# Dealing the prompt's chunks to five blocks: 5, 7, 7, 7, 6 in place of 4, 7, 7, 7, 7

## The chip, the core and the metric

The kernel runs on one core of a Trainium2 chip. The metric is device time in microseconds (us); a run's time is one execution of the whole kernel, and medians of several runs are compared. PE is TensorE's matmul, PEld its weight load, DVE is VectorE, ACT is ScalarE, POOL is GpSimd, SP is SyncE, whose queue issues most transfers. The profiled execution is one run by itself.

## What is computed

One layer of a streaming encoder for two groups of tokens: a sample of 64 tokens that continues a running stream, and a prompt of 2048 tokens with 16 meta tokens in front. Each row of 1024 values is normalised, projected to 11144 columns, and sent through three branches; their gated sum is projected again, added to the input and normalised:

```python
P   = x @ w_in                       # 11144 columns
y_b = branch_b(P columns) * silu(gate_b columns)      # b in rwkv7, s5, mlstm
m   = sum_b sigmoid(P_merge_b + b_merge_b) * (y_b @ w_br_b)
x   = layer_norm(DN_ALPHA * x + m @ w_out)
```

RWKV-7 carries a 64 x 64 state in each of 12 heads, S5 a complex diagonal state in 32 groups, mLSTM a 192 x 192 memory in each of 4 heads. Every branch is causal by token, so tokens can be worked in chunks with the state carried over. All states are outputs, for the sample and for the prompt. Everything is float32.

## The kernel before, in words

The 64 + 16 + 2048 = 2128 tokens lie in one row, cut into five **blocks** (BLOCKS, L36, a number of 64-token chunks for each). Block 0 holds the sample, the meta tokens and four chunks of the prompt: T = 336 columns. The others hold seven chunks, 448 columns. Activations are held with features on the partitions and tokens along the free dimension, so that T is the width of nearly every instruction.

A float32 product is made of three matmuls on parts (mm3, L427): weight and activation are each split into a high and a low part, and for each of eight slices of 128 input features there are three matmuls, 24 for 128 output columns. There are 63 such projections per block (psum tile d) and 24 for the merge gates (gate_pass, L1493, mostly psum tile f). In block 0 (`first`) the weights come from w_in: split_w (L392) loads a tile (wraw, graw), casts it on ACT (L403), subtracts on POOL (L404) and stores both parts in memory (wsp, L409); load_w (L414) of later blocks loads these parts (L423). Buffers: three of wraw, four each of whi and wlo, two each of graw, ghi and glo. The normalised activations xh, xl of a block stand in one set of buffers, loaded from xT for each block after the first.

RWKV works in **slots** of 64 tokens: block 0 has a slot for the sample, one for the meta tokens (48 of its 64 places empty) and one for each chunk, six in all; the other blocks have seven. For each of six head pairs, rw_front (L512) makes the operands and inverts a triangular block for all slots at once (L615, L617, 31 steps whatever the number of slots), rw_prep (L628) makes slot matrices with small matmuls, and rw_back (L715) runs the state from slot to slot (L723, L741) and normalises.

mLSTM works in **token tiles** of up to 128 (Block.tiles). In block 0 they are 64 (sample), 16 (meta), 128, 128; in the others 128, 128, 128, 64. ml_tiles (L976) runs through them one after the other, for each of two head pairs, and carries the memory Cst; the scale factors per tile are made in ml_gates (L834). ln_first (L205) normalises block 0 in the same tiles, all of them kept in memory before the first projection; ln_stage (L168) does it for the next block while a block runs, and stores xT. Both load a tile's rows with one transfer (src_rows, L158). S5 (s5_block, L1310) works on T/8 columns with scans; its tables are made once, in block 0's time (s5_setup, L1119, mostly L1128).

The order of the work is not that of the program text alone. Generators of the three branches are interleaved by weights (mix, L1449; MIXES, L1671), and a planner then places every instruction on its engine with simulated times. The last RWKV pair, the second mLSTM head pair and S5 of block 0 are finished in the next block's time (pend, mpend, spend).

After the last block, merge_pass (L1503) works on the 2112 tokens without the meta rows in groups of 768, 768 and 576 (TBS, L1504): branch outputs (yraw) and gates (th) are loaded for each group, one transfer for each block that the group touches (segs), then three branch products and the output product (L1556) and the last norm (norm) follow. Its groups end at 768 and 1536; block borders lie at 320, 768, 1216 and 1664 of the same count.

Of the kernel before, what the change touches and what calls it, by code (L numbers as in the profile page):

```python
# [21 lines left out]
NMETA = 16  # L22
NSAMP = 64
NTOK = NSAMP + NMETA + SEQ
# [8 lines left out]
DN_ALPHA = 2 ** 0.25  # L33
O_RW, O_RG, O_S5U, O_S5G, O_MQ, O_MK, O_MV, O_MIF, O_MO, O_MZ, O_MG = (
    0, 2432, 3200, 3712, 4224, 4992, 5760, 6528, 6536, 7304, 8072)
BLOCKS = (4, 7, 7, 7, 7)  # L36
CH = 64
C2 = 0.5 * math.exp(-0.5)
LN05 = math.log(0.5)
# [2 lines left out]
HPO = 300  # L42
TMAX = CH * max(BLOCKS)
RMAX = 448
# [3 lines left out]
class Block:  # L48
    def __init__(self, i, t0, nch):
        self.i, self.t0, self.nch = i, t0, nch  # L50
        self.first = i == 0
        pre = NSAMP + NMETA if self.first else 0
        self.T = pre + CH * nch
        self.nslot = nch + (2 if self.first else 0)
        self.R = self.nslot * CH
        self.last = i == len(BLOCKS) - 1
        if self.first:
            self.seqs = [(0, NSAMP), (NSAMP, self.T - NSAMP)]
            self.pads = [(0, 0, 80), (80, 128, self.T - 80)]
            self.shift = [(0, 0, 64, 0), (64, 64, 16, 1), (80, 128, self.T - 80, 1)]  # L60
            self.tiles = [(0, 64), (64, 16)]
        else:
            self.seqs = [(0, self.T)]
            self.pads = [(0, 0, self.T)]
            self.shift = [(0, 0, self.T, 0)]
            self.tiles = []
        t = pre
        while t < self.T:
            n = min(128, self.T - t)
            self.tiles.append((t, n))  # L70
            t += n


def make_blocks():
    out, t = [], 0
    for i, n in enumerate(BLOCKS):
        b = Block(i, t, n)
# [6 lines left out]
def tile_trunk(ctx: ExitStack, tc: tile.TileContext, I, O, dbg=None, parts=("rw", "s5", "ml", "mg")):  # L84
    nc = tc.nc
# [21 lines left out]
    def pt(pool, shape, tag, dt=F32, bufs=None):  # L107
        uid[0] += 1
        kw = {} if bufs is None else {"bufs": bufs}
        return pool.tile(list(shape), dt, tag=tag, name=f"{tag}_{uid[0]}", **kw)  # L110
# [3 lines left out]
    def psum(shape, tag):  # L114
        return pt(ps, shape, tag, bufs=PSB[tag])
# [9 lines left out]
    def flat(tag, n, dt=F32, bufs=None):  # L125
        return pt(op, (128, n), tag, dt, bufs=bufs)

    def cut(t, off, shape):
        n = 1
        for x in shape[1:]:  # L130
            n *= x
        v = t[:shape[0], off:off + n]
        if len(shape) == 3:
            v = v.rearrange("p (a b) -> p a b", b=shape[2])
        elif len(shape) == 4:
            v = v.rearrange("p (a b c) -> p a b c", b=shape[2], c=shape[3])
        elif len(shape) == 5:
            v = v.rearrange("p (a b c d) -> p a b c d", b=shape[2], c=shape[3], d=shape[4])
        return v
# [15 lines left out]
    SB = 4  # L155
    NX = 1536

    def src_rows(b, lo, n):  # L158
        g = b.t0 + lo
        if g < NSAMP:  # L160
            return I["x_sample"][0, g:g + n, :]
        g -= NSAMP
        if g < NMETA:
            return I["meta"][g:g + n, :]
        g -= NMETA
        return I["x_prompt"][0, g:g + n, :]

    def ln_stage(b):  # L168
        for i, (lo, n) in enumerate(b.tiles):
            X = flat("X", NX)  # L170
            x = cut(X, 0, (128, D))
            nc.sync.dma_start(x[:n], src_rows(b, lo, n))
            st = pt(lnp, (128, 2, 6), "st", bufs=2)
            for j in range(2):
                V.bn_stats(st[:n, j, :], x[:n, 512 * j:512 * j + 512])
            mv = pt(lnp, (128, 2), "mv", bufs=2)
            V.bn_aggr(mv[:n], st[:n])
            ve = pt(lnp, (128, 1), "ve", bufs=2)
            V.tensor_scalar(ve[:n], mv[:n, 1:2], 1.0, LN_EPS, ALU.mult, ALU.add)
            rs = pt(lnp, (128, 1), "rs", bufs=2)  # L180
            rsqrt(lnp, rs[:n], ve[:n], (n, 1), "lq")
            nb = pt(lnp, (128, 1), "nb", bufs=2)
            V.scalar_tensor_tensor(nb[:n], mv[:n, 0:1], -1.0, rs[:n], ALU.mult, ALU.mult)
            S.activation(x[:n], x[:n], AF.Identity, bias=nb[:n], scale=rs[:n])
            for j in range(2):
                p = psum((128, 4, 128), "o")
                for k in range(4):
                    c0 = 512 * j + 128 * k
                    PE.transpose(p[:, k, :n], x[:n, c0:c0 + 128], ident[:n, :n])
                for k in range(0, 4, 2):  # L190
                    kk = 4 * j + k
                    xg = cut(X, 1024, (128, 2, 128))
                    hi = cut(X, 1280, (128, 2, 128)).bitcast(F32R)
                    for i in range(2):
                        V.tensor_scalar(xg[:, i, :n], p[:, k + i, :n], pcol("in_g", kk + i), pcol("in_b", kk + i),
                                        ALU.mult, ALU.add)
                    S.copy(hi[:, :, :n], xg[:, :, :n])
                    G.tensor_tensor(xg.bitcast(F32R)[:, :, :n], xg[:, :, :n], hi.bitcast(F32)[:, :, :n], ALU.subtract)
                    nc.sync.dma_start(xT_d[b.i][0, :, kk:kk + 2, lo:lo + n], hi.bitcast(F32)[:, :, :n])
                    nc.scalar.dma_start(xT_d[b.i][1, :, kk:kk + 2, lo:lo + n], xg[:, :, :n])  # L200
            yield
# [3 lines left out]
    def ln_first(b):  # L205
        nt = len(b.tiles)
        xs = []
        mv = pt(lnp, (128, nt, 2), "mv4")
        V.memset(mv, 1.0)
        for i, (lo, n) in enumerate(b.tiles):  # L210
            X = flat("va", NVA) if i == 0 else flat("X", NX) if i == 3 else pt(
                rp, (128, NSL, 2, 128), "AT", bufs=2).rearrange("p c h t -> p (c h t)")
            x = cut(X, 0, (128, D))
            nc.sync.dma_start(x[:n], src_rows(b, lo, n))
            st = pt(lnp, (128, 2, 6), "st", bufs=2)
            for j in range(2):
                V.bn_stats(st[:n, j, :], x[:n, 512 * j:512 * j + 512])
            V.bn_aggr(mv[:n, i], st[:n])
            xs.append((x, cut(X, 1024, (128, 4, 128))))
        ve = pt(lnp, (128, nt), "ve4")  # L220
        V.tensor_scalar(ve, mv[:, :, 1], 1.0, LN_EPS, ALU.mult, ALU.add)
        rs = pt(lnp, (128, nt), "rs4")
        rsqrt(lnp, rs, ve, (128, nt), "lq4")
        nb = pt(lnp, (128, nt), "nb4")
        V.scalar_tensor_tensor(nb, mv[:, :, 0], -1.0, rs, ALU.mult, ALU.mult)
        cur["xh"], cur["xl"] = ([pt(big, (128, TMAX), f"{nm}{k}", F32R) for k in range(KD)] for nm in ("xh", "xl"))
        for i, (lo, n) in enumerate(b.tiles):
            x, xg = xs[i]
            if str(i) in NV:
                V.tensor_scalar(x[:n], x[:n], rs[:n, i:i + 1], nb[:n, i:i + 1], ALU.mult, ALU.add)  # L230
            else:
                S.activation(x[:n], x[:n], AF.Identity, bias=nb[:n, i:i + 1], scale=rs[:n, i:i + 1])
            for j in range(2):
                p = psum((128, 4, 128), "o" if j or not NP else "d")
                for k in range(4):
                    c0 = 512 * j + 128 * k
                    PE.transpose(p[:, k, :n], x[:n, c0:c0 + 128], ident[:n, :n])
                for k in range(4):
                    kk = 4 * j + k
                    hi, l = cur["xh"][kk][:, lo:lo + n], cur["xl"][kk][:, lo:lo + n]  # L240
                    S.activation(hi, p[:, k, :n], AF.Identity, bias=pcol("in_b", kk), scale=pcol("in_g", kk))
                    V.tensor_scalar(xg[:, k, :n], p[:, k, :n], pcol("in_g", kk), pcol("in_b", kk), ALU.mult, ALU.add)
                    G.tensor_tensor(l, xg[:, k, :n], hi.bitcast(F32), ALU.subtract)
        for j, nm in enumerate(("xh", "xl")):
            for k in range(KD):
                nc.sync.dma_start(xT_d[b.i][j, :, k, :], cur[nm][k].bitcast(F32)[:, :b.T])
# [65 lines left out]
    def pcol(name, j=0, n=1):  # L312
        return PT[:, col[name] + j:col[name] + j + n]
# [5 lines left out]

    load_rows(0, 2, ["rk"])  # L320
    ln_first(blocks[0])
    load_rows(2, len(rows_spec), ["kk", "L", "Bc"])

# [1422 lines left out]
```

## Time and profile before

| | |
|---|---|
| median of 3 runs | 4168.24 us (4159.67 to 4174.69) |
| profiled execution | 4180.76 us, of which the span from the first to the last instruction is 4179.0 us |
| PE busy | 3882.8 us, 93% |
| DVE busy | 2513.7 us, 60% |
| ACT busy | 1206.4 us, 29% |
| POOL busy | 672.2 us, 16% |
| moved by DMA | 834.88 MB, 200 GB/s on the mean |
| mean granted clock of TensorE | 0.958 |

Busy is the time in which an engine had an instruction; matmuls are pipelined, so one lasts longer than the distance to the next, and a stream's pace is read from the starts. The granted clock is a share of 2.4 GHz, the mean of a stretch over the levels 1.2 and 2.4 GHz. In the 40 slices of the page, POOL is busy in the first six (block 0) and the last six (merge), where weights are split.

### The profile page before, as it was taken

What the parts mean: (1) busy time and instruction counts of PE and PEld (TensorE: products, weight loads), DVE (VectorE), ACT (ScalarE), POOL (GpSimd) and SP (SyncE); (2) the same over time, 40 slices, a digit from 0 to 9 for tenths busy, and PEclk for the clock granted to TensorE, in tenths of its full rate; (3) what the DMA queues carried; (4) which work ended last, traced back from release to release, by engine and by line L of the source; (5) the groups of instructions that cost most, each with busy time, mean ns of one, the idle gap of its engine ahead of it and who ended that gap; (6) DMA issues with size and microseconds to landing.
All of it is one profiled execution on the core that took longest, in us unless ns stands there. A gap on an engine that the chain in (4) does not pass through costs nothing.

```text
span 4179.0 us, 78015 instructions
## 1 busy us (share of the span) xinstructions
PE 3882.8 (93%) x27729; PEld 3321.6 (79%) x27729; DVE 2513.7 (60%) x8212; ACT 1206.4 (29%) x2655; POOL 672.2 (16%) x978
## 2 busy tenths in 40 slices
PE   6888779899999899999899999999999998999997
PEld 6777567687888788788778888778888786999997
DVE  6556887566566555656545656564666554357476
ACT  5334332233222222223222322232322232222222
POOL 5544322000000000001000001000000000232334
PEclk9999879899999899999999999999999999999999
DMA  8999647665666755666655656566565556566565
GB/s 265 314 288 313 214 132 230 181 200 184 189 212 199 238 180 182 194 186 209 190 191 176 199 184 214 174 214 204 176 204 186 158 169 183 169 197 194 160 179 161
DMA packets 803860, 834.88 MB, mean 200 GB/s; under 512 B 220246, under 2 KB 557374, under 8 KB 803470
## 3 DMA queue, kind: packets, MB, share of 16 engines
q1 hardware_dynamic: 725582, 756.61, 58.4%
q10 hardware_dynamic: 77888, 73.28, 6.0%
q8 instruction: 219, 3.59, 0.4%
q14 instruction: 171, 1.40, 0.1%
HBM read 633.92 MB, written 197.79 MB: 199 GB/s over the span
## 4 chain that ended last, share of the span: by engine, by line
PE 61%; DMA 11%; DVE 9%; SPq 2%; ACT 2%; issue 1%; POOL 1%; ACTq 0%; DVEq 0%; POOLq 0%
PE d L432 25%; PE f L432 8%; PE z L1556 7%; PE g L1556 3%; DMA xT<-X 2%; PE py L723 1%; DMA ghi<-wsp 1%; PE tr L578 1%; PE d L1411 1%; DMA E<-rd 1%; PE tr L697 1%; PE tr L705 1%; DMA Uin<-Ud 1%; PE o L1005 1%; PE o L1368 1%
## 5 line engine op out<-in xcount | busy, mean ns | idle before, releaser
L432 PE MATMUL d<-xh,whi 128*128 128x448 f32 (+1 forms) x2520 | 951.4, 378 | 31.4 <-ACT X L935 9.6
L432 PE MATMUL d<-xh,wlo 128*128 128x448 f32 (+1 forms) x2520 | 940.0, 373 | 7.5 <-POOL wlo L404 6.9
L432 PE MATMUL d<-xl,whi 128*128 128x448 f32 (+1 forms) x2520 | 933.8, 371 | 0.0
L432 PEld LDWEIGHTS d<-xh,whi 128*128 128x128 f32 x2520 | 489.1, 194 | 89.6 <-issue 14.0
L432 PEld LDWEIGHTS d<-xh,wlo 128*128 128x128 f32 x2520 | 488.3, 194 | 60.8 <-POOL wlo L404 11.2
L432 PEld LDWEIGHTS d<-xl,whi 128*128 128x128 f32 x2520 | 489.1, 194 | 44.5 <-issue 8.5
L404 POOL TENSOR_TENSOR wlo<-wraw,whi 128x512 fp32r<-128x512 f32 (+1 forms) x310 | 399.5, 1298 | 541.8 <-ACT whi L403 505.0
L432 PE MATMUL f<-xh,ghi 128*128 128x448 f32 (+1 forms) x912 | 351.2, 385 | 42.3 <-DMA ghi<-wsp 17.0
L432 PE MATMUL f<-xh,glo 128*128 128x448 f32 (+1 forms) x912 | 346.5, 380 | 14.5 <-POOL glo L404 10.3
L432 PE MATMUL f<-xl,ghi 128*128 128x448 f32 (+1 forms) x912 | 340.5, 373 | 0.0
L403 ACT CAST whi<-wraw 128x512 fp32r<-128x512 f32 (+1 forms) x310 | 179.2, 585 | 400.5 <-PE z L1556 111.5
L615 DVE TENSOR_TENSOR Ztmp<-Uin,Z 128x60 f32<-128x60 f32 (+24 forms) x930 | 214.0, 230 | 99.5 <-DMA Uin<-Ud 84.4
L432 PEld LDWEIGHTS f<-xh,ghi 128*128 128x128 f32 x912 | 180.0, 197 | 72.6 <-ACT ghi L403 18.6
L617 DVE TENSOR_TENSOR Z<-Z,Ztmp 128x60 f32<-128x60 f32 (+24 forms) x930 | 213.5, 230 | 15.6
L432 PEld LDWEIGHTS f<-xh,glo 128*128 128x128 f32 x912 | 179.6, 197 | 41.5 <-POOL glo L404 14.2
L1556 PE MATMUL z<-ya,whi 128*128 128x384 f32 (+1 forms) x784 | 192.1, 325 | 0.0
L432 PEld LDWEIGHTS f<-xl,ghi 128*128 128x128 f32 x912 | 180.5, 198 | 13.4 <-issue 2.0
L942 DVE SCALAR_TENSOR_TENSOR X<-X,PT 128x448 f32<-128x448 f32 (+1 forms) x180 | 123.0, 683 | 55.0 <-ACT X L940 53.0
L1556 PEld LDWEIGHTS z<-ya,whi 128*128 128x128 f32 x784 | 138.1, 189 | 0.2 <-issue 0.2
L1500 ACT ACTIVATE gt<-f,hbm 128x448 f32<-128x448 f32 (+1 forms) x114 | 69.9, 613 | 200.4 <-PE f L432 142.0
L1556 PE MATMUL z<-ya,wlo 128*128 128x384 f32 (+1 forms) x384 | 124.9, 325 | 0.0
L1556 PE MATMUL z<-yb,whi 128*128 128x288 f32 (+1 forms) x512 | 119.8, 316 | 2.7 <-DVE lq2i L251 1.8
(724 smaller groups left out, 6866.9 us busy)
## 6 DMA issues: line engine op xcount, KB each, us to landing
whi<-wsp SPq DMA_DIRECT2D x504, 256.0 KB
wlo<-wsp SPq DMA_DIRECT2D x504, 256.0 KB
ghi<-wsp SPq DMA_DIRECT2D x192, 256.0 KB
glo<-wsp SPq DMA_DIRECT2D x192, 256.0 KB
wraw<-in_w_in_dram SPq DMA_DIRECT2D x126, 256.0 KB
wsp<-whi SPq DMA_DIRECT2D x126, 256.0 KB
wsp<-wlo SPq DMA_DIRECT2D x126, 256.0 KB
gt<-gt SPq DMA_DIRECT2D x96, 224.0 KB
```

Of the source, the lines that this page charges most:

```text
L403: S.copy(h[:, :n, :M], raw[:, :n, :M])
L404: G.tensor_tensor(l[:, :n, :M], raw[:, :n, :M], h.bitcast(F32)[:, :n, :M], ALU.subtract)
L432: PE.matmul(p, a[k], c, start=i == 0, stop=i == 3 * KD - 1)
L578: i = PE.matmul(p[h][:, c].rearrange("p (j t) -> p j t", j=2), bk[h][:, c0 + c, :], AQ[hs[h], c0 + c], start=True, stop=True)
L615: V.tensor_tensor(t3, Uin[:, j:j + 1, j + 1:32].to_broadcast((128, m, n)), Z[:, 0:m, j:j + 1].to_broadcast((128, m, n)), ALU.mult)
L617: V.tensor_tensor(Z[:, 0:m, j + 1:32], Z[:, 0:m, j + 1:32], t3, ALU.add)
L697: PE.matmul(p[hs[h], c], Tt[hs[h], c0 + c, :], AR[hs[h], c0 + c], start=True, stop=True)
L705: PE.matmul(p[hs[h], c], PX[hs[h], c0 + c, 0, :], AT[hs[h], c0 + c, h, :], start=True, stop=True)
L723: i = PE.matmul(o, a, x, start=start, stop=stop, skip_group_check=True)
L942: V.scalar_tensor_tensor(acc[:, :w], raw[:, j:j + w], pcol("conv_w", 12 * j + ti), acc[:, :w], ALU.mult, ALU.add)
L1500: S.activation(t[:, :T], p[:, :T], AF.Tanh, scale=0.5, bias=hbm[:, j:j + 1])
L1556: PE.matmul(p, a[k], c[:, sl], start=i == 0, stop=i == n - 1)
```

## The change

The list becomes (5, 7, 7, 7, 6). Block 0 then has 400 columns and seven slots, the last block 384 columns and six slots; the blocks in between keep their size and begin one chunk later. Block 0's tiles after the sample are no longer cut at the end of the meta rows: they are 64, 128 (16 meta rows and 112 of the prompt), 128 and 80; the last block's are 128, 128, 128. A tile can thus have its rows in two inputs; load_rows_x issues a transfer for each and takes the place of src_rows in ln_stage and ln_first.

```diff
-BLOCKS = (4, 7, 7, 7, 7)
+BLOCKS = (5, 7, 7, 7, 6)
...
-            self.tiles = [(0, 64), (64, 16)]
+            self.tiles = [(0, 64)]
...
-        t = pre
+        t = NSAMP if self.first else 0
...
-    def src_rows(b, lo, n):
...
+    def load_rows_x(x, b, lo, n):
+        parts_ = ((0, I["x_sample"][0]), (NSAMP, I["meta"]), (NSAMP + NMETA, I["x_prompt"][0]))
+        g, i = b.t0 + lo, 0
+        for (s0, src), s1 in zip(parts_, (NSAMP, NSAMP + NMETA, NTOK)):
+            m = min(g + n, s1) - max(g + i, s0)
+            if m > 0 and g + i >= s0:
+                nc.sync.dma_start(x[i:i + m], src[g + i - s0:g + i - s0 + m, :])
+                i += m
...
-            nc.sync.dma_start(x[:n], src_rows(b, lo, n))
+            load_rows_x(x, b, lo, n)
```

Block borders in the count without meta rows move to 384, 832, 1280 and 1728.

## Rows read from the trace of the kernel before

**Rows 1.** The page: busy shares, and the group of weight loads of one kind.
```profile
PE 3882.8 (93%) x27729; PEld 3321.6 (79%) x27729; DVE 2513.7 (60%) x8212; ACT 1206.4 (29%) x2655; POOL 672.2 (16%) x978
...
L432 PEld LDWEIGHTS d<-xh,whi 128*128 128x128 f32 x2520 | 489.1, 194 | 89.6 <-issue 14.0
```
**Rows 2.** Stretches: length, busy PE, PEld, DVE, ACT, POOL, clock, DMA share, GB/s.
```profile
30.00:440.00 410.00, 352.39 (x2339) 314.68 (x2337) 238.93 (x708) 161.97 (x352) 199.91 (x219) 0.93 0.95 305
440.00:683.00 243.00, 183.07 (x1341) 145.63 (x1341) 201.86 (x860) 84.82 (x236) 72.06 (x107) 0.78 0.56 172
...
2860.00:3430.00 570.00, 556.16 (x4223) 461.82 (x4223) 350.69 (x1159) 160.22 (x361) 29.88 (x84) 0.99 0.58 178
...
3567.00:4179.00 612.00, 578.98 (x3594) 572.33 (x3592) 360.14 (x657) 148.19 (x244) 226.43 (x180) 0.98 0.59 174
```
**Rows 3.** The same stretches, L432 alone: length, busy PE, PEld, clock, DMA.
```profile
30.00:440.00 410.00, 303.25 (x1631) 270.77 (x1629) 0.93 0.95 305
440.00:683.00 243.00, 95.79 (x457) 84.12 (x457) 0.78 0.56 172
...
2860.00:3430.00 570.00, 389.12 (x1680) 310.83 (x1680) 0.99 0.58 178
3430.00:3567.00 137.00, 88.29 (x360) 67.23 (x360) 0.96 0.63 189
```
**Rows 4.** The chain's shares in 440:700, 2860:3430, 3430:3570 and 3570:4179.
```profile
by line: DVE sB L1128 7.8%; PE d L432 6.4%; DMA s5wo<-sB 3.5%; DVE X L942 3.4%; DVE Ztmp L615 2.9%; PE o L1277 2.3%; DVE Z L617 2.2%; PE f L432 2.2%; DVE sA L1128 2.0%; issue 1.7%; DMA Kd<-tab 1.2%; PE tr L578 1.1%; DMA Uin<-Ud 1.0%; PE tr 
...
by line: PE d L432 45.2%; PE f L432 4.9%; DMA E<-rd 2.9%; PE py L723 2.6%; PE tr L578 2.5%; PE tr L705 1.8%; PE tr L697 1.7%; DMA Uin<-Ud 1.5%; PE o L1005 1.2%; issue 1.2%; DMA Tt<-Zd 1.1%; PE o L1375 1.1%; PE tr L711 1.1%; PE d L1411 1.1%;
...
by line: PE f L432 20.5%; DMA ghi<-wsp 18.7%; PE d L432 14.9%; DMA glo<-wsp 10.3%; SPq L633 2.3%; DMA Uin<-Ud 2.3%; PE py L723 2.1%; DVE Ztmp L615 2.0%; PE z L1556 2.0%; PE o L1005 2.0%; DVE Z L617 1.9%; PE o L1000 1.8%; issue 1.5%; PE tr L
...
by line: PE z L1556 48.9%; PE g L1556 23.0%; DMA yraw<-yml 4.2%; issue 2.4%; DVE st L1590 1.7%; DVE xn L1599 1.7%; DVE lq2a L255 1.6%; DMA wraw<-in_w_out_dram 1.6%; DVE lq2a L254 1.5%; DMA xr<-xT 1.4%; DVE xn L1600 1.4%; DVE rs L260 1.4%; P
```
**Rows 5.** Pieces of the chain: start, length, what.
```profile
1494.33 9.85 PE d L432 x48
...
3466.02 4.54 DMA glo<-wsp
...
3567.33 134.41 PE z L1556 x768
...
4046.95 47.97 PE z L1556 x360
```
**Rows 6.** PE's groups by shape, whole span: count, busy, mean ns; idle before.
```profile
L578 PE MATMUL tr<-AQ,BK 64*128 64x128 f32 x816 | 91.4, 309 | 4.0 <-DVE BK L560 2.5 <-POOL BK L561 1.5
...
L1005 PE MATMUL o<-Cst,t 128*64 128x193 f32 x40 | 10.2, 335 | 0.0
...
L723 PE MATMUL py<-Ss,AQ 64*64 64x64 f32 x96 | 8.2, 249 | 0.2 <-ACT Ss L789 0.2
...
L1065 PE MATMUL o<-ident,NK 64*128 64x64 f32 x30 | 4.6, 244 | 0.0
```
**Rows 7.** What SP's queue waited for in 3430:3567: total, times, longest.
```profile
SPq L423 <- PE f L432: 39.5, 13, 6.5
```
**Rows 8.** PE in order of time in 305:311 (block 0): start, length.
```profile
304.74 0.32 PE L432 MATMUL f<-xh,glo 128*128 128x336 f32 x1
...
308.94 0.31 PE L432 MATMUL d<-xh,wlo 128*128 128x336 f32 x1
```
**Rows 9.** A DVE group in 440:683: count, busy, mean ns.
```profile
L604 DVE SCALAR_TENSOR_TENSOR sg<-sg,d 128x336 f32<-128x336 f32 x3 | 1.5, 497 | 1.4 <-ACT sg L603 1.4
```
**Rows 10.** The same group in 2860:3567.
```profile
L604 DVE SCALAR_TENSOR_TENSOR sg<-sg,d 128x448 f32<-128x448 f32 x6 | 3.7, 613 | 1.8 <-ACT sg L603 1.8
```
**Rows 11.** Transfers in 30:440.
```profile
DMA packets 138059, 124.85 MB, mean 305 GB/s; under 512 B 18015, under 2 KB 102968, under 8 KB 138019
```
**Rows 12.** The start in order of time, DVE's statistics of two tiles.
```profile
6.89 1.26 DVE L217 BATCH_NORM_STATS2 st<-AT 16x6 f32<-16x512 f32 x2
...
8.31 1.27 DVE L217 BATCH_NORM_STATS2 st<-AT 128x6 f32<-128x512 f32 x2
```

More of the change, by code (lines that the diff above doesn't have):

```diff
@@ L156, in tile_trunk @@
     NX = 1536
-    def src_rows(b, lo, n):
[L159 to L166, printed above, removed]
+    def load_rows_x(x, b, lo, n):
[6 more added lines that the diff above has]
+                i += m
     def ln_stage(b):
@@ L213, in ln_first @@
             x = cut(X, 0, (128, D))
-            nc.sync.dma_start(x[:n], src_rows(b, lo, n))
+            load_rows_x(x, b, lo, n)
             st = pt(lnp, (128, 2, 6), "st", bufs=2)
```

## The prediction, written before the result

> **What bounds the kernel now.** I read the page's busy shares first, then cut the span into stages, then asked in each stage which wait ends last. TensorE is busy for 93% of the span [rows 1], so its idle places decide what work can be moved for nothing. The stages show where these are [rows 2]: the reader compares the PE column with the length of each stretch. From 30 to 440 us PE idles 410 − 352 = 58 us, and there the DMA engines are taken for 95%; from 440 to 683 us it idles 243 − 183 = 60 us, the granted clock is 0.78, a mixture of the 1.2 and 2.4 GHz levels, and VectorE is busy for 202 of the 243 us. From 2860 to 3430 us PE idles only 14 of 570 us.
>
> The first two stretches are block 0: the matmuls of L432 in them are 1631 + 457 [rows 3], which is the 87 × 24 = 2088 of one block (63 projections and 24 merge gates, 24 matmuls each). The next two are the last block (2040 of its 2088). So block 0 waits for something other than PE, and the last block waits for PE. The chain says the same [rows 4]: in 440 to 700 us its first name is VectorE's L1128 (the tables of S5), from 2860 to 3430 us it is L432 with 45%. From 3430 to 3570 us the chain alternates between L432 and the weight loads (ghi, glo).
>
> **The change part by part.** One chunk of 64 tokens moves from the last block to block 0. Block 0 goes from 336 to 400 columns and from 6 to 7 slots, the last block from 448 to 384 columns and from 7 to 6 slots. Totals stay (336 + 448 = 400 + 384), so the worth of the change is the difference between the price of a chunk where PE is the limit and its price where it is not.
>
> *Off the last block, PE work.* (a) Projections and gates. 48 matmuls of 448 columns follow each other in 9.85 us, 205 ns each; in the merge, 768 of 384 columns take 134.4 us, 175 ns each; 360 of 288 columns take 48.0 us, 133 ns each [rows 5]. The spacing follows the columns. 2088 × (205 − 175) = 62.6 us, of which 360 × 30 = 10.8 us lie after 3430 us. (b) One slot of the RWKV work. The twelve groups of small matmuls with one entry per slot (L578, L723, L697, L705, L689, L684, L711, L668, L659) are busy for 507 us over 6 + 4 × 7 = 34 slots [rows 6], 14.9 us a slot. (c) Two mLSTM tiles: 448 tokens are tiles of 128, 128, 128, 64; 384 are three of 128; there are two head pairs. The eleven groups of 64-row tiles are busy for 71.9 us in ten passes [rows 6], 7.2 us each, 14.4 us for two. (d) Transposes that go from four to three per pass and S5's eight columns fewer: a few us, left at nothing. The sum is 62.6 + 14.9 + 14.4 = 92 us.
>
> At a spot of the Trainium skill this sum would be far smaller. Its page TensorE: Matmul & The Clock Gate (Back-to-back issue gap) gives for a stream of weight loads and matmuls about 81 ns per matmul at 128 columns and about 131 ns at 512, a slope of 0.13 ns per column; as an estimate from that page, 64 columns would be worth 8.3 ns and (a) 17 us. The rows above have 0.44 to 0.47 ns per column, so the measurement decides and (a) stays.
>
> How much of the 92 us shortens the block? Not more than all. The least is half: PE is busy for 97.6% from 2860 to 3430 us, but the matmuls named in the chain's row there add up to 63% (small groups left out); the rest holds round trips (E, Uin, Tt from memory [rows 4]) that other generators' matmuls cover and that show up when the cover gets thinner. After 3430 us the load of the next gate's weights waits for the matmuls that read the buffer (39.5 us in 13 waits [rows 7]) and lands some 4.5 us later [rows 5], so a shorter matmul group shortens about half of each round. VectorE, busy for 351 of 570 us, is late next, but far off. I take 80%, nearest to the busy share: −73 us, between −46 and −92.
>
> *Onto block 0.* PE gets 2088 × 29 ns (64 columns at 155.6/336 = 0.46 ns each: 27 spacings in 4.20 us [rows 8]) = 60.6 us, plus 14.9 us for the slot: 76 us, against 118 us of idle time. By the counts of rows 3, 78% of it, 59 us, falls into 30 to 440 us where 58 are idle, 17 us into 440 to 683 us where 60 are idle (at the low level of the clock it would be up to 34). The cover is the DMA stream in the first stretch and VectorE in the second; if PE had to pay, it would be 76 us.
> VectorE: the same instruction (L604) takes 497 ns at 336 columns and 613 ns at 448 [rows 9, 10], 1.04 ns a column, 66 ns for 64. Some 300 instructions per block have that width (read from the code): 20 us. In the first stretch VectorE is busy for only 239 of 410 us, so that part is hidden; in the second it is the limit, and its share by time (243 of 653 us) is 7 us. I take it as exposed.
> DMA: 64 more columns of x, xT, gates and branch outputs are about 2.5 MB (gates 3072 × 64 × 4 = 0.8 MB, x and both halves of xT 0.8 MB, branches about 0.9 MB). At the stretch's 305 GB/s [rows 11] that is 8 us, exposed because the queue has no room there.
> Another 5 us are for PE where it happens to be the later one. Sum: 7 + 8 + 5 = 20 us, between +5 and +60.
>
> *The rest.* The tile of 16 meta rows grows into a full one across the border, and a last tile of 80 rows comes in: block 0's four tiles stay four. The small tile was not cheap for being small: statistics of 16 rows take 1.26 us, of 128 rows 1.27 us [rows 12]. The border tile needs two loads; block 0's start gets 1 us, between 0 and 3. Of block 0's deferred work (second head pair of mLSTM, last RWKV pair, S5) block 1 gets 64 columns more on a full PE: +3 us, between 0 and 8. The blocks in between shift by one chunk and keep size. In the merge the second group of 768 tokens is now cut from three blocks instead of two: 16 + 24 + 16 = 56 more transfers, most of them pieces of 64 columns, on SP's and ACT's queues. PE is busy for 579 of 612 us there and the waits for yraw are 4.2% of it, 26 us [rows 4], so +2 us, between 0 and 8. Those on ACT's queue stand before the casts of ACT, which is busy for 148 of 612 us.
>
> Sum: −73 + 20 + 1 + 3 + 2 = −47 us. The profiled execution took 4180.8 us (span 4179.0), so 4134 us; it stands 12.5 us above the median of the runs, 4168.2, so I predict 4121 us. A change below 0.3%, 12.5 us, can't be told from none here.
>
> **Rivals.**
> *Block 0 hides nearly everything* (over −70 us): PE really fits, VectorE's 7 us fall between its waits, and the last block gives 92: −92 + 8 = −84, 4084 us. For it: 118 us of idle PE. Against: both stretches have a second resource near its limit.
> *The weight load sets the spacing.* A load of 128 columns lasts 194 ns on the mean [rows 1]. Were a matmul of 384 columns held to that, (a) would be 2088 × 11 = 23 us and the block would lose 23 + 29 = 52 × 0.8 = 42 us: −42 + 26 = −16, 4152 us. Against: the merge's 288 columns run at 133 ns [rows 5]. Small.
> *The DMA stream takes over all of it.* The extra bytes, VectorE and a thinner cover cost 45 us in block 0 and the last block gives only its half: −46 + 45 + 6 = +5, 4173 us, no change.
> *Slower: the weight buffers tie PE and DMA together in block 0.* A new weight tile is loaded, cast on ACT, subtracted on POOL, and both parts are stored; its buffers (four of whi and wlo, two of ghi and glo) come free only after the matmuls that read them. If every group of 24 matmuls holds them 0.7 us longer and the DMA engines pause meanwhile, PE's 59 us add to the 410 us instead of filling them, the 17 to 34 us add to the second stretch, with VectorE's 7: +83 to +100 us. That decides from the point where block 0 grows by more than 67 us; at +90 it is −73 + 90 + 6 = +23, 4191 us. For it: 95% DMA with PE idle in pieces, which is how such a ring looks. Against: a share of 95% leaves no pause to be longer.
> That the change doesn't do what it says can't be: the column counts follow from the list. But the order of all instructions is planned anew, and that alone may move the end by some 10 us either way.
>
> **How the numbers follow.** Forecast (−15 to −70 us) 0.62; block 0 hides nearly everything 0.15; weight load 0.03; no change 0.12; slower 0.08. Range: 4080 us (the second case, a little beyond) to 4165 us (the upper end of the forecast and most of the third); about 0.2 lie outside. Faster by over 0.3%: 0.62 + 0.15 + 0.02 = 0.79; within: 0.12; slower: 0.09.
>
> **What would show it.** L432 at about 175 ns in the last block and 183 ns in block 0; the first 448-wide matmul about 20 us later than 683 us; the stretch from there to the merge's first matmul about 70 us shorter; PE's idle time in block 0 well below 118 us, VectorE near its limit in the last third. I would be wrong if block 0 grew by over 67 us, or if the last block kept its length with PE idle.

## The result and the profile after

The changed kernel takes 4117.3 us (median of 4 runs, 4111.6 to 4120.8) against 4164.0 us before in the same group of runs: ratio 0.9883, 95% interval 0.9864 to 0.9902, 47 us less. Run again in the group of the experiments it came to 0.9906 (0.9886 to 0.9925), 39 us. The forecast was −47 us and 4121 us. The profiled execution took 4111.6 us, 69 us less than that of before; of these some 22 us are chance, for the profiled execution of before was slower than its median and this one was the fastest of its four.

In the changed kernel's text one line is gone above the places named, so L432 is L431, L1556 is L1555, and so on. The page's busy shares; PE is busy for 43 us less in all:

```profile
PE 3839.6 (93%) x27644; PEld 3330.6 (81%) x27644; DVE 2483.5 (60%) x8127; ACT 1201.7 (29%) x2626; POOL 686.3 (17%) x974
```

The stretches of [rows 2] in the changed kernel, the last two of them with the new borders (length, busy PE, PEld, DVE, ACT, POOL, granted clock, DMA share, GB/s):

```profile
30.00:440.00 410.00, 380.07 (x2426) 345.63 (x2425) 259.44 (x738) 173.69 (x359) 205.58 (x226) 0.98 0.94 303
440.00:683.00 243.00, 193.32 (x1394) 159.16 (x1394) 204.38 (x837) 86.58 (x227) 70.94 (x107) 0.85 0.62 190
...
2844.00:3372.00 528.00, 504.67 (x3847) 448.89 (x3846) 293.71 (x1087) 141.73 (x340) 32.27 (x81) 0.96 0.66 206
3372.00:3506.00 134.00, 102.16 (x831) 87.47 (x830) 65.80 (x235) 38.56 (x91) 4.28 (x7) 0.84 0.53 147
3506.00:4110.00 604.00, 577.66 (x3592) 571.49 (x3591) 359.66 (x658) 148.38 (x244) 229.35 (x180) 0.99 0.60 177
```

Against [rows 2] the reader sees PE filling its idle time in block 0 (352 to 380 us, 183 to 193 us), at a granted clock that rose from 0.93 to 0.98 and from 0.78 to 0.85, and a new weak place: from 3372 us to the merge PE is busy for 102 of 134 us at a clock of 0.84. In the 134 us ahead of the merge of before it was 118 us at 0.96:

```profile
3433.00:3567.00 134.00, 118.39 (x771) 95.22 (x771) 62.33 (x237) 38.27 (x91) 0.80 (x2) 0.96 0.63 187
```

Where a block ends is read from counts: 2088 matmuls of L432 (L431) belong to each. L432 before, and then L431 after, each cut where four blocks are done and where the merge begins (length, busy PE, PEld, clock, DMA):

```profile
0.00:2844.00 2844.00, 1862.70 (x8352) 1523.67 (x8352) 0.95 0.67 209
2844.00:3567.00 723.00, 488.88 (x2088) 386.66 (x2088) 0.98 0.60 184
```
```profile
0.00:2845.00 2845.00, 1895.95 (x8352) 1555.23 (x8352) 0.97 0.68 211
2845.00:3505.50 660.50, 430.26 (x2089) 372.81 (x2088) 0.94 0.63 194
```

8352 is 4 × 2088. The first four blocks, one of them now a chunk longer, end 1 us later than before. The last block takes 660 us instead of 723, and the merge 604 instead of 612. So in this pair of executions the chunk costs about nothing where it went and gives 62 us where it came from. Cut in the same way after each of the first four blocks, with all engines (columns as in [rows 2]), before and after:

```profile
0.00:681.50 681.50, 542.16 (x3693) 465.37 (x3695) 461.14 (x1658) 263.21 (x628) 287.81 (x381) 0.88 0.80 251
681.50:1399.00 717.50, 684.72 (x5255) 567.84 (x5255) 452.32 (x1671) 198.64 (x458) 44.34 (x114) 0.98 0.66 202
1399.00:2140.00 741.00, 700.76 (x5121) 579.92 (x5122) 419.32 (x1429) 195.22 (x431) 39.57 (x105) 0.95 0.62 193
2140.00:2844.00 704.00, 682.63 (x4938) 564.01 (x4938) 403.40 (x1383) 196.86 (x433) 43.17 (x111) 0.98 0.62 193
```
```profile
0.00:677.00 677.00, 576.92 (x3793) 508.35 (x3793) 479.55 (x1642) 273.72 (x616) 290.53 (x375) 0.93 0.81 257
677.00:1403.70 726.70, 694.91 (x5437) 574.69 (x5438) 460.62 (x1693) 205.53 (x470) 48.47 (x120) 0.99 0.66 201
1403.70:2149.00 745.30, 702.88 (x5122) 578.59 (x5121) 419.77 (x1429) 196.35 (x431) 40.31 (x105) 0.96 0.62 193
2149.00:2845.00 696.00, 681.37 (x5036) 561.87 (x5033) 404.35 (x1384) 197.40 (x435) 41.05 (x107) 0.99 0.63 194
```

Block 0 has the chunk and is not longer: 677 us after 682, and PE's idle time in it fell from 139 to 100 us. Block 1 is 9 us longer.

### The profile page after: what moved, and what is told of

Its sections match the earlier page's. It is cut to its first block, busy times and chain, and to the rows that moved or that the text cites. A ratio compares the mean times of both kernels' runs of the same rounds, so it can differ in the third digit from the quotient of the medians.

```text
span 4109.7 us, 77783 instructions
## 1 busy us (share of the span) xinstructions
PE 3839.6 (93%) x27644; PEld 3330.6 (81%) x27644; DVE 2483.5 (60%) x8127; ACT 1201.7 (29%) x2626; POOL 686.3 (17%) x974
## 4 chain that ended last, share of the span: by engine, by line
PE 64%; DVE 14%; DMA 13%; SPq 3%; ACT 2%; issue 2%; POOL 1%; ACTq 0%; DVEq 0%; POOLq 0%
PE d L431 27%; PE f L431 9%; PE z L1555 7%; PE g L1555 4%; PE py L722 2%; PE tr L577 2%; DMA xT<-X 2%; DVE Ztmp L614 1%; DMA glo<-wsp 1%; DVE Z L616 1%; PE tr L696 1%; PE tr L704 1%; PE o L1004 1%; PE d L1410 1%; DMA ghi<-wsp 1%
## 5 line engine op out<-in xcount | busy, mean ns | idle before, releaser
L431 PE MATMUL d<-xh,whi 128*128 128x448 f32 (+2 forms) x2520 | 947.1, 376 | 55.7 <-DVE zo L1085 12.7
L431 PE MATMUL d<-xh,wlo 128*128 128x448 f32 (+2 forms) x2520 | 935.0, 371 | 4.3 <-POOL wlo L403 3.3
L431 PE MATMUL d<-xl,whi 128*128 128x448 f32 (+2 forms) x2520 | 929.2, 369 | 0.0
L431 PEld LDWEIGHTS d<-xh,whi 128*128 128x128 f32 x2520 | 484.4, 192 | 108.1 <-issue 22.2
L431 PEld LDWEIGHTS d<-xh,wlo 128*128 128x128 f32 x2520 | 483.6, 192 | 48.8 <-issue 9.6
L431 PEld LDWEIGHTS d<-xl,whi 128*128 128x128 f32 x2520 | 484.8, 192 | 36.4 <-issue 7.6
L431 PE MATMUL f<-xh,ghi 128*128 128x448 f32 (+2 forms) x912 | 347.4, 381 | 22.6 <-DMA ghi<-wsp 11.3
L431 PE MATMUL f<-xh,glo 128*128 128x448 f32 (+2 forms) x912 | 342.0, 375 | 6.3 <-DMA glo<-wsp 3.4
L431 PE MATMUL f<-xl,ghi 128*128 128x448 f32 (+2 forms) x912 | 335.9, 368 | 0.0
L431 PEld LDWEIGHTS f<-xh,ghi 128*128 128x128 f32 x912 | 177.3, 194 | 44.7 <-DMA ghi<-wsp 13.3
L431 PEld LDWEIGHTS f<-xh,glo 128*128 128x128 f32 x912 | 177.0, 194 | 25.7 <-DMA glo<-wsp 7.1
L1555 PE MATMUL z<-ya,whi 128*128 128x384 f32 (+1 forms) x784 | 190.7, 323 | 0.0
L431 PEld LDWEIGHTS f<-xl,ghi 128*128 128x128 f32 x912 | 177.7, 195 | 11.6 <-issue 1.8
L941 DVE SCALAR_TENSOR_TENSOR X<-X,PT 128x448 f32<-128x448 f32 (+2 forms) x180 | 125.2, 695 | 53.7 <-ACT X L939 51.4
L1555 PEld LDWEIGHTS z<-ya,whi 128*128 128x128 f32 x784 | 137.4, 188 | 0.0
L698 DVE COPY XV<-tr 64x512 f32<-64x512 f32 (+2 forms) x60 | 36.8, 614 | 148.1 <-ACT XV L697 147.4
L1555 PE MATMUL z<-ya,wlo 128*128 128x384 f32 (+1 forms) x384 | 124.5, 324 | 0.0
L1555 PE MATMUL z<-yb,whi 128*128 128x288 f32 (+1 forms) x512 | 119.7, 316 | 3.6 <-DVE lq2i L250 1.8
```

What stands on the lines that cost most here:

```text
L431: PE.matmul(p, a[k], c, start=i == 0, stop=i == 3 * KD - 1)
L941: V.scalar_tensor_tensor(acc[:, :w], raw[:, j:j + w], pcol("conv_w", 12 * j + ti), acc[:, :w], ALU.mult, ALU.add)
L1555: PE.matmul(p, a[k], c[:, sl], start=i == 0, stop=i == n - 1)
```

## The experiments

Twelve kernels, in three groups, each timed against the kernel before in its group (4178.6, 4180.1 and 4181.6 us). The changed kernel's own 0.9906 of the first group is what the doses are compared with. Its interval is 0.002 wide to either side, some 8 us, and against the 0.9883 of the first measurement every price below would be 10 us higher; so 10 us between two of these numbers say little. Gains and prices in us are taken from the ratios here.

**The change once more.**

> The changed kernel once more, as the measure for the others of this group. All theories: 0.986 to 0.990 of the kernel before, about 4117 us, with the stretch from the last block's first projection to the merge's first matmul about 62 us shorter than before and block 0 as long as before within 6 us.

Measured: 4139.4 us, 0.9906 (0.9886 to 0.9925). The ratio is a little above the range expected and the intervals of the two groups overlap. The first four blocks ended at 2858 us, later than in the other two profiles; the last block took 662 us, as in the first profile. Block 0 took 680 us, within the 6 us expected; block 1 took 740 us, 22 more than before.

**The tiles alone.**

```diff
-BLOCKS = (5, 7, 7, 7, 6)
+BLOCKS = (4, 7, 7, 7, 7)
```

> The chunks stay 4, 7, 7, 7, 7; only the token tiles of block 0 cross the border of meta rows and prompt (64, 128, 128, 16 for 64, 16, 128, 128). Theory A (a chunk of PE work moves from where PE is the limit to where it idles): no change, within 8 us of the kernel before. Theory B (the gain is in the tiles): at least a third of the gain, 15 us or more faster.

Measured: 4199.2 us, 1.0045 (1.0028 to 1.0062): 19 us slower. Theory B is gone, the gain is not in the tiles; but theory A's "no change" missed as well. L432 of this kernel, in the cuts of above:

```profile
0.00:2857.00 2857.00, 1859.82 (x8352) 1516.25 (x8352) 0.95 0.68 208
2857.00:3582.00 725.00, 486.53 (x2088) 384.60 (x2088) 0.98 0.61 183
```

The loss that the profile shows is in the first four blocks (2857 us against 2844), the last is as long as before (725 against 723). Cut by blocks, block 0 takes 688 us (682 before) and block 1 732 (717); so a longer block 1, which the change has too, comes without the chunk as well.

**The chunk from another block.** BLOCKS is (5, 7, 7, 6, 7), (5, 6, 7, 7, 7) or (5, 7, 6, 7, 7), and nothing else differs from the change.

> The chunk is taken from block 3 instead of the last: 5, 7, 7, 6, 7. Theory A: the same PE work leaves a block that is full of PE work to its end, so 50 to 75 us faster than before, at least as fast as the change; block 3 is shorter by 60 to 85 us and the last block as long as before. Theory C (what got shorter is the last block's end, where the last head pair runs without cover): within 12 us of the kernel before.

> The chunk is taken from block 1: 5, 6, 7, 7, 7. Theory A: 40 to 70 us faster than before; a little less than from block 3, since block 1 begins beside the end of the S5 tables. Theory C: within 12 us of the kernel before.

> The chunk is taken from block 2: 5, 7, 6, 7, 7. Theory J: like block 3, since a block in the middle has the next block's matmuls behind its last chain: 0.978 to 0.984 of the kernel before. If the place of the short block matters for another reason, the position of the plan among them, it lies with the change at 0.987 to 0.992.

Measured: from block 3 4094.1 us, 0.9803 (0.9783 to 0.9823); from block 1 4109.6 us, 0.9849 (0.9819 to 0.9878); from block 2 4118.8 us, 0.9844 (0.9826 to 0.9862). Theory C is gone: with a last block as long as before the gain is larger, 82, 63 and 65 us against 39. Block 3's gain lies above the range that theory A gave it; block 2's ratio lies just above what theory J gave and below the other case, so the place matters in some other way too. The profiles show where: the short block 3 is 82 us shorter than before, the short block 2 some 50 us (690 after 741) and the short block 1 39 us (678 after 717), with the granted clock at 0.98 (as before), 0.93 (0.95 before) and 0.96 (0.98 before). Before, PE idled 21, 40 and 33 us in these blocks; the one most full of PE work gave most. That this is the cause was not tested. L431 of the kernel with the short block 3, by the counts first three blocks, block 3, last block; then PE in order of time at the merge's begin:

```profile
0.00:2142.00 2142.00, 1410.31 (x6261) 1167.87 (x6261) 0.96 0.70 216
2142.00:2764.00 622.00, 428.59 (x2091) 368.38 (x2092) 0.98 0.67 212
2764.00:3469.00 705.00, 484.23 (x2090) 386.26 (x2089) 0.99 0.63 188
```
```profile
3469.09 0.37 PE L431 MATMUL d<-xh,glo 128*128 128x448 f32 x1
3469.29 0.52 PE L1555 MATMUL z<-ye,whi 128*128 128x384 f32 x2
```

Block 3 took 704 us in the profile of before (from 2140 us to 2844 us, by the same counts) and takes 622 here: 82 of the 92 us of the forecast's sum (74 and 78 us less than the 696 and 700 us of the same block in the two profiles of the change). The merge's first matmul follows the last gate's without a gap. So it does in the kernel before, where the last step of the last RWKV pair (ACT So L803) is done 19 us earlier:

```profile
3547.91 0.26 ACT L803 COPY So<-tr 87x128 f32<-87x128 f32 x1
...
3566.96 0.37 PE L432 MATMUL d<-xh,glo 128*128 128x448 f32 x1
3567.17 0.52 PE L1556 MATMUL z<-ye,whi 128*128 128x384 f32 x2
```

In the change there is a gap:

```profile
3479.18 0.34 PE L431 MATMUL d<-xh,glo 128*128 128x384 f32 x1
3479.44 1.53 PE L696 MATMUL tr<-AR,Tt 64*64 64x128 f32 x24
3482.84 1.09 PE L704 MATMUL tr<-AT,XV 64*64 64x128 f32 x16 [1.87 <-DVE XV L698]
...
3491.48 1.55 PE L722 MATMUL py<-XV,AT 128*64 128x64 f32 x24 [0.39 <-DVE Hw L740]
...
3500.55 0.87 PE L624 MATMUL tr<-ident,sq 128*128 128x128 f32 x3 [6.04 <-DVE sq L765]
...
3505.52 1.01 PE L1555 MATMUL z<-ye,whi 128*128 128x384 f32 x2 [2.17 <-ACT So L802]
```

The gates are used up at 3479 us, and for 26 us PE has only the last RWKV pair (L696 to L802), which goes on step after step between PE, VectorE and ScalarE, before the merge begins. The gates end 634 us after the block's begin (723 before), the pair 660 us (704 before): the one came forward by 89 us, the other by 44.

**Work added to block 0 and to block 3 of the change.** Gates multiplied twice (in block 3 by b.i == 3 in place of b.first); S5 products made twice; weight parts stored twice.

```diff
-            mm3(p[:, :T], wh, wl, T)
+            for _ in range(2 if b.first and j < 12 else 1):
+                mm3(p[:, :T], wh, wl, T)
```

> A dose of PE work into block 0 of the changed kernel: the first 12 of its merge gates are multiplied twice (288 more matmuls of 400 columns, 53 us at 183 ns). The changed kernel itself ran at 0.988 and 0.991 of the kernel before. Theory A (PE idles in block 0 behind DMA and VectorE): the whole kernel grows by less than 20 us, to at most 0.994. Rival D (the change used up the room, or the weight buffers tie PE and DMA together): 35 to 53 us more, 0.998 to 1.002.

> The same dose into block 3 of the changed kernel (288 more matmuls of 448 columns, 59 us at 205 ns). Theory A: PE is the limit there, so 45 to 59 us more, 1.000 to 1.004 of the kernel before. Rival E (the chain of round trips, not PE, sets a full block's length): less than 30 us, below 0.996.

Measured: in block 0 4133.3 us, 0.9898 (0.9871 to 0.9924), which is −0.0008 or −3 us against the change (+7 against its first measurement): nothing that can be told. In block 3 4187.2 us, 1.0016 (1.0003 to 1.0029), +0.0110 or 46 us of 59. By the kernel's time rivals D and E are gone. The reader sees in the stretches of block 0 what the dose did there: PE from 193 to 225 us in the second, at a clock of 0.92, while in the first the DMA engines are taken for 0.87, not 0.94, and VectorE is busy for 290 us, not 259. The order was planned anew around it. (Columns as in [rows 2].)

```profile
30.00:440.00 410.00, 374.16 (x2451) 339.56 (x2449) 290.03 (x983) 167.01 (x357) 184.69 (x219) 0.96 0.87 270
440.00:683.00 243.00, 224.64 (x1599) 187.32 (x1601) 187.94 (x656) 90.20 (x233) 75.78 (x102) 0.92 0.69 209
```

But block 0 did not swallow the dose by itself. Its last projection or gate ends at 756 us, 77 to 80 us later than in the two profiles of the change; blocks 1 and 2 behind it are together 68 to 75 us shorter. Blocks 0, 1 and 2 with the dose:

```profile
0.00:757.00 757.00, 670.88 (x4592) 587.33 (x4595) 543.45 (x1894) 294.86 (x674) 296.30 (x389) 0.95 0.80 243
757.00:1451.00 694.00, 671.18 (x5218) 560.98 (x5214) 413.93 (x1483) 189.56 (x422) 41.47 (x112) 0.98 0.66 204
1451.00:2161.00 710.00, 685.55 (x4838) 563.56 (x4832) 406.36 (x1388) 195.53 (x425) 40.35 (x99) 0.98 0.64 197
```

Block 0 has 800 matmuls more than in the change, of which the dose is 288; the others are work that the change does in blocks 1 and 2. Against the first profile of the change PE idles 14 us less in block 0, 9 less in block 1 and 18 less in block 2. So PE's idle time took the dose, but the smaller part of it lies in block 0.

L431 of block 3 with the dose (2088 + 288 matmuls); without it, in the first group's profile of the change, block 3 took 700 us:

```profile
2146.00:2926.00 780.00, 551.39 (x2376) 436.19 (x2376) 0.99 0.56 175
```

Block 3 grew by 80 us and the last block behind it was 636 instead of 662 us long, 54 us in the two. So a full block, too, hands part of its dose on; block 0 has more blocks behind it that can take it. A dose in block 1 or 2, which would part the two readings (idle time in block 0, or room in the blocks behind), was not run.

```diff
-            cmul(BL[:, 0], BL[:, 1], be(0), be(1), pr(0), pr(1), tb[:, 0:8])
-            cmul(CL[:, 0], CL[:, 1], ce(0), ce(1), pe(0, 9), pe(1, 9), tb)
+            for _ in range(2):
+                cmul(BL[:, 0], BL[:, 1], be(0), be(1), pr(0), pr(1), tb[:, 0:8])
+                cmul(CL[:, 0], CL[:, 1], ce(0), ce(1), pe(0, 9), pe(1, 9), tb)
```

> A dose of VectorE work into block 0 of the changed kernel: two complex products of the S5 tables are made twice (192 more instructions of 128 and 144 columns at some 0.30 us, 58 us in all). The prediction's term (VectorE is the limit from 440 to 683 us): 35 to 58 us more, 0.998 to 1.003 of the kernel before. Rival F (VectorE has room, since block 1 begins while the tables are still being made): less than 20 us more, at most 0.994.

```diff
                     nc.sync.dma_start(wsp_d[keep][k // 4, j], t.bitcast(F32))
+                    if tag == "g" and keep < O_MG + 128 * 16:
+                        nc.sync.dma_start(spare_d[len(wsp_d) % 2, k // 4, j], t.bitcast(F32))
...
+    spare_d = pt(dram, (2, 2, 2, 128, 4, 128), "spare")
```

> A dose of transfers into block 0 of the changed kernel: the weight parts of the first 16 gates are stored a second time (64 transfers of 256 KB, 16.8 MB, 55 us at 303 GB/s). The prediction's term (the DMA queue has no room from 30 to 440 us): 35 to 55 us more, 0.998 to 1.003 of the kernel before. Rival G (what the stream loses is given back in the stretch after 440 us, where the DMA engines are taken for 62%): less than 20 us more, at most 0.994.

Measured: VectorE's dose 4159.2 us, 0.9955 (0.9940 to 0.9970), +0.0049 or 20 us of 58; the transfers' dose 4155.8 us, 0.9947 (0.9932 to 0.9961), +0.0041 or 17 us of 55. By their ratios both lie between the two cases that were set against each other (at most 0.994 and at least 0.998), at about a third of the dose, or half of it against the change's first measurement (30 and 27 us): neither is the sole limit there. Block 0 itself ends at 702 us with VectorE's dose and at 715 us with the transfers' (677 and 680 in the change), 22 to 39 us later. The stretch of block 0 after 440 us with VectorE's dose, then its stretch before 440 us with the transfers' dose:

```profile
440.00:683.00 243.00, 185.22 (x1276) 151.76 (x1275) 210.09 (x867) 80.65 (x205) 71.74 (x101) 0.78 0.55 168
```
```profile
30.00:440.00 410.00, 359.99 (x2258) 320.77 (x2257) 226.62 (x601) 159.42 (x329) 187.00 (x213) 0.96 0.99 319
```

VectorE is busy for 210 of 243 us, hardly more than the 204 of the change, and the rest moved on (from 683 to 800 us it is busy for 84 us, 67 without the dose). The DMA engines go from 0.94 to 0.99 and carry 319 instead of 303 GB/s, and VectorE's and PE's work of the stretch falls behind.

**The end of the last block.**

```diff
-            mm3(p[:, :T], wh, wl, T)
+            for _ in range(2 if b.last and j >= 18 else 1):
+                mm3(p[:, :T], wh, wl, T)
```

> A dose of PE work at the end of the changed kernel's last block: its last 6 merge gates are multiplied twice (144 more matmuls of 384 columns, 25 us at 175 ns). Theory J (the last block's matmuls run out before the chain of the last head pair, which is what the forecast of 73 us lost): less than 10 us more than the change, at most 0.993 of the kernel before. Rival K (PE is the limit to the end of the block): 18 to 25 us more, 0.995 to 0.997.

Measured: 4146.7 us, 0.9913 (0.9886 to 0.9941), +0.0007 or 3 us against the change, with an interval that reaches to +0.0035 (15 us) and leaves out the full dose of 25 us (0.9906 + 0.0060). The change was timed in another group; against its first measurement the dose costs 13 us, which is neither theory J's "less than 10" nor rival K's 18 to 25. The profile of this run takes the middle: the last block lasts 677 us (662 in the change's of the first group), while the last gate now ends 8 us ahead of the merge instead of 26:

```profile
3531.56 0.34 PE L431 MATMUL d<-xh,glo 128*128 128x384 f32 x1
3535.09 0.52 PE L624 MATMUL tr<-ident,sq 128*128 128x128 f32 x3 [3.19 <-DVE sq L765]
...
3539.70 1.01 PE L1556 MATMUL z<-ye,whi 128*128 128x384 f32 x2 [2.16 <-ACT So L802]
```

So part of the 25 us goes into the gap for nothing, as theory J has it; that all of it does is not shown, and the profile's 15 us speak against it. That the end of the last block waits for the pair is read from the rows above and not from this dose.

**Tiles cut at chunk borders**, in the change and in the kernel with the short block 3:

```diff
-            self.tiles = [(0, 64)]
+            self.tiles = [(0, 64), (64, 80)]
...
-        t = NSAMP if self.first else 0
+        t = 144 if self.first else 0
```

> The changed kernel with block 0's token tiles cut at chunk borders: 64, 80 (16 meta rows and one chunk), 128, 128 in place of 64, 128, 128, 80. The same number of tiles and matmuls. Theory H (where the tiles are cut costs time, as the tiles alone did with a last tile of 16 rows): 10 to 20 us faster than the change, 0.984 to 0.987 of the kernel before. Rival I (what the tiles alone cost was the tile of 16 rows at the end of block 0, or the plan of the order; a cut is worth nothing): within 8 us of the change, 0.988 to 0.992.

> The short block third from the front of the last two (5, 7, 7, 6, 7, as in the run that took the chunk from block 3, 0.980) with tiles cut at chunk borders (64, 80, 128, 128): the version that should be best if both help. Theory H: 10 to 20 us faster than 0.980, 0.975 to 0.978. Rival I: 0.978 to 0.982.

Measured: in the change 4134.6 us, 0.9885 (0.9867 to 0.9904), not told apart from the change. That is in rival I's range; the interval's lower end touches theory H's. With the short block 3 4086.5 us, 0.9770 (0.9752 to 0.9788), the fastest kernel of the study, 96 us below the kernel before. It lies in theory H's range, but its interval touches that of the other tiles (0.9783 to 0.9823), so what the cut gives there isn't settled. Why the tiles alone cost 19 us stays open: the tile of 16 rows at the end of block 0, or the order that was planned for it.

## Why the prediction was right

The mechanism, PE work from a block that is full of it to one where PE idles, is shown by the change's own profiles (block 0 takes the chunk and ends 5 and 2 us earlier than before, with 39 and 36 us less idle time of PE; it ends at 677 to 685 us in all nine profiles that have the chunk there and no dose in block 0, after 682 before; the last block is 62 us shorter) and by the kernels with another short block, which gain without a shorter last block. The pair of doses gives the prices at the kernel's end, −3 us of 53 in block 0 and 46 of 59 in block 3; block 0 owes its low price in part to the blocks behind it. The sum of −47 us met the measured −47 and −39, but two of its terms were off in opposite ways, so that it met to the microsecond is luck.

- **(a), the matmuls.** Right. In the last block 23 matmuls of 384 columns take 3.99 us, 173 ns each; in block 0 there are 130 spacings from 102.81 to 126.47 us, 182 ns each at 400 columns. 175 and 183 were forecast, so the spacing follows the columns and not the time of a weight load. That rival is gone. So is the estimate from the Trainium skill's page TensorE: Matmul & The Clock Gate (Back-to-back issue gap), 8.3 ns for 64 columns: from 205 ns at 448 columns [rows 5] to 173 at 384 it is 32 ns.

```profile
3141.68 3.99 PE f L431 x23
```
```profile
102.81 0.35 PE L431 MATMUL f<-xh,ghi 128*128 128x400 f32 x1
...
126.47 0.35 PE L431 MATMUL d<-xl,whi 128*128 128x400 f32 x1
```

- **80% of 92 us, −73 us off the last block.** The factor was about right for block 3 (46 of 59 us of the dose is 78%; the block lost 82 of 92), and too high for the last: 62 us, 68%. The step that failed is the one about the end of the block. The forecast let part of the work be lost to thinner cover and to weight loads (its 63% for the matmuls named in the chain's row is 64%, which changes nothing); what happened is that the last gate came forward by 89 us, nearly the whole 92, and the last RWKV pair by 44, so that the merge waits 26 us for that pair, which before was done 19 us ahead of it.
- **+20 us in block 0.** Too high; the first four blocks together grew by 1 us in one profile and 14 in the other, where 20 + 1 + 3 had been put. Block 0 itself ended 5 and 2 us earlier, and the first matmul of 448 columns starts 3 and 7 us later, not the 20 that were to show it; from there to the merge it is 64 and 53 us less than before, where 70 were to show it. Block 1 grew by 9 and 22 us instead of 3, but with the tiles alone it grew by 15. The forecast put the clock at nothing: PE's busy time in block 0 grew by 35 us where 76 us of work had been put, at a granted clock of 0.93 instead of 0.88. Where the clock is at its low level (0.50 from 678 to 680 us, before; the lines below), matmuls of 336 columns follow each other at 280 ns, not at the 156 of [rows 8]. VectorE's 7 us: its work did grow by 23 us, near the 20 forecast, but 20 of them (239 to 259) lie before 440 us, where it has room, and 2.5 after; a share by time was the wrong key. DMA's 8 us: the share before 440 us is 0.94 after 0.95, and the stretch after 440 us carries 190 instead of 172 GB/s; what had no room in the one can have gone into the other. Even of pure doses a third to a half shows up in the time. PE's 5 us: nothing that can be seen.

```profile
678.14 0.48 PE L432 MATMUL d<-xh,whi 128*128 128x336 f32 x1
...
679.82 0.48 PE L432 MATMUL d<-xh,whi 128*128 128x336 f32 x1
```

- **The merge, +2 us.** 604 us after 612. The 56 more transfers cost nothing that can be seen; as the second profile of the change has 608 us there and those of other cuts 603 to 608, I don't read the 8 us as a gain.
- **The slower rival** (weight buffers tie PE and DMA together) would have needed 67 us in block 0, and with the chunk block 0 did not grow. The dose of 53 us of the very matmuls that hold those buffers did make block 0 77 to 80 us longer, with the DMA engines taken for less (0.87 for 0.94 before 440 us), but the kernel's time did not show it; whether the buffers had a part in that stays open.

In the profiled pair the forecast took 11 us too much off the last block and put 23 too much onto the first four and 10 onto the merge; the 22 us that remain are what this pair's difference (69 us) has above that of the medians (47 us). The second profile has 13 us more in the first four blocks and 4 more in the merge, so the terms are resolved to some 10 us, and not better, and the sum came closer than its parts. How much the tiles take away from the gain is open: they cost 19 us alone, and with a different cut the change was not told apart from itself.

## What to carry to other kernels

Work of one size has a different price in each stage: read the idle time of the limiting engine by stage, and move work to where it idles, but don't take the last stage as the giver if its work covers a serial chain: block 3 gave 82 us, the last one 39 to 47 for the same chunk. A resource at 95% in one stretch need not be the only limit if the plan can carry its work into the next: 55 us of transfers cost 17 to 27 us. A dose tells such a price in one run; where it went is read from the blocks behind it.

## What was not expected

- The granted clock of TensorE rose in block 0 when PE got more work: 0.78 to 0.85 from 440 to 683 us with the change, 0.92 with the dose, while PE's idle time there fell from 60 to 50 and 18 us. At the end of the last block it was 0.68 from 3440 us to the merge, where PE was busy for 36 of 66 us.
- The changed kernel ended its first four blocks at 2845 us in one profile and at 2858 us in another, so an effect of 10 us needs the timed ratio, not a profile.
- The place of the short block in the middle matters more than the forecast had any term for: 82 us from block 3, 63 and 65 from blocks 1 and 2. With the short block 3 the last block, unchanged in size, was also 18 us shorter (705 for 723 us); with the short block 2 it took 713 us, with the short block 1 725. Why was not tried.
